# Input table of an S5 layer: its powers stored by group instead of by time step

## The chip, the cores and the metric

The kernel runs on one core of a Trainium2 chip. The metric is device time in microseconds (us), the median of the timed runs. The engines are TensorE (PE, with its weight loads PEld), VectorE (DVE), ScalarE (ACT), GpSimd (POOL) and SyncE (SP). Here POOL and SP mostly issue transfers (DMA).

## The reference, cut to what matters

A two-layer backbone on 1024 latent tokens with 256 context tokens and 1024 channels. Layer 0 has 48 groups of a bidirectional S5 recurrence (16 channels and 64 complex states per group and direction) beside an FNet part; layer 1 has pooling and a short convolution. What the change touches is the S5 recurrence of layer 0:

```
lam_bar = exp(lam * step)
b_bar   = ((lam_bar - 1) / lam)[..., None] * complex(b_re, b_im)
bu      = einsum('btgh,gph->btgp', u, b_bar)        # input to the state
s[t]    = lam_bar * s[t-1] + bu[t]                  # scan over time, both directions
y       = einsum(s.real, c_re) - einsum(s.imag, c_im)
```

All arithmetic is float32; large products are made of three products of exact high and low parts.

## The kernel before, in words

Time is cut into chunks of 8 steps. For a chunk the state's input is one matrix product: the chunk's 8 x 16 inputs times a matrix that holds, for every channel h and step s, B scaled by the power of lam_bar that belongs to s. A group's matrix has 128 columns (16 h x 8 s) and 128 rows (two directions x 64 states), for the real and the imaginary part.

`s5_prelim` (from L401) makes the powers `pw`, shaped [128, 4, 9, 48]: real part, two sums, imaginary part; powers 0 to 8; groups. Its inner function `tables(0)` copies powers 0 to 7 on ScalarE into `pwb`, six copies of 64 x 384 (three parts, two directions; one direction with the powers reversed). `tables(1)` makes `pwc` and `acf` in the same way.

`bl_task` (L493) takes four groups at a time; there are twelve such tasks. Its vector part is five VectorE operations of 128 x 512: a product into `blp`, two products into `bl`, a subtraction and an addition in `bl`. The three products read `pwb` through `W` (L502), a view [4 groups, 16 h, 8 s] in which h has step zero, and B through a view in which s has step zero. Its tensor part transposes `bl` on TensorE (L515, eight transposes into `pt`), evacuates it on ScalarE to `bltw` and stores it with a POOL transfer to `bltd`, from which `bl_load` (L964) takes it later as `blt`. `bl` has two buffers. `cl_task` (L521) does likewise for the output matrices, with `pwc`.

The order of the work is written out by hand (`manual_schedule`); each engine runs its instructions in that order. In `layer0`, from L972, a loop over six channel tiles m makes the S5 inputs: 48 products of 512 columns for the latent tokens (L360, into `acc`) and 24 of 256 columns for the context (into `uc`). Tiles 0 and 1 have their long products done before the loop; from m = 2 on the weights' high and low parts are made one tile ahead (`whi` on ScalarE, `wlo` on VectorE). `fill` (L949) is called between the products, five times per tile from m = 2 on and once at the end of m = 1: it runs the tensor part of the task started two calls before and then starts the vector part of a new one. The twelve `bl_task`s come first, then the twelve `cl_task`s. `tables(0)` stands before this loop (L923); `tables(1)` stands in it at m = 1 (L985), and the memory of the `bl` tiles is free only after it.

Behind the loop come the chunk inputs (`bl_mm`, L1018, with loads of `blt` and `ub` on the SP queue), the scan over chunks on VectorE, beside gate projections on TensorE, the S5 outputs, FNet, and then the projections of the rest of layer 0 and of layer 1.

Of the kernel before, what the change touches and what calls it, by code (L numbers as in the profile page):

```python
# [9 lines left out]
F32 = mybir.dt.float32  # L10
# [4 lines left out]
PSUM = bass.MemoryType.PSUM  # L15
DRAM = bass.MemoryType.DRAM

P = 128
# [9 lines left out]
NG = 48  # L28
EPS = 1e-6

# ------------------------------------------------------------------ constants that depend on shapes
# [17 lines left out]
def fold_index():  # L49
    """Order of the 512 time steps of the folded half: t = 8 j + s, held as s * 128 + j."""  # L50
    lin = list(range(128, 576)) + list(range(0, 64))
    return np.array([8 * (i % 128) + i // 128 for i in lin])
# [130 lines left out]
class Builder:  # L183
# [8 lines left out]
    # ---------------------------------------------------------------- small helpers  # L192
    def tick(self):
        """Between small dependent operations, the larger ones that wait for their turn (a number: that many later)."""
        self.cnt -= 1
        if self.inter and self.cnt == 0:
            self.cnt = -1000000
            while self.inter:
                x = self.inter.pop(0)
                if isinstance(x, int):  # L200
                    self.cnt = x
                    break
                x()
# [44 lines left out]
    # ---------------------------------------------------------------- streamed weights  # L248
# [51 lines left out]
    def w_issue(self, upto=-1):  # L300
        """Loads: those that the ring has room for or that have a place of their own, and all up to the given one."""
        while self.issued < len(self.jobs):
            i = self.issued
            t = self.place.get(i)
            if t is None:
                if (self.live == self.R or self.hold) and i > upto:
                    break
                t = self.wp.tile([P, 1024], F32, tag="raw", name="raw", bufs=self.R)
                self.live += 1
            self.nc.sync.dma_start(t[:, :self.jobw[i]], self.jobs[i])  # L310
            self.raw[i] = t
            self.issued += 1
# [12 lines left out]
    def w_split(self, name, eng=None, hi=None, lo=None, parts=1, c0=0, c1=None):  # L325
        """The stationary tile's exact high and low parts (columns c0 .. c1, of those that were left)."""
        if name in self.split:
            if c0 == 0:
                return self.split[name]
            hi, lo = self.split[name]  # L330
        i, raw = self.w_raw(name)
        w = self.jobw[i]
        if hi is None:
            hi = self.wp.tile([P, 1024], F32R, tag="whi", name="whi", bufs=2)
        if lo is None:
            lo = self.wp.tile([P, 1024], F32R, tag="wlo", name="wlo", bufs=2)
        for c in range(parts):
            sl = slice(max(c0, w // parts * c), min(c1 or w, w // parts * (c + 1)))
            self.act(hi[:, sl], raw[:, sl])
            self.sub(lo[:, sl], raw[:, sl], hi[:, sl].bitcast(F32), eng)  # L340
        if c1 is None:
            self.w_done(i)
        self.split[name] = (hi, lo)
        return hi, lo
# [6 lines left out]
    # ---------------------------------------------------------------- main product  # L351
    def mm3(self, outs, hi, lo, rhs, nk, hook=None):
        """outs: [(psum, first col, end col)]; rhs(k) -> (hi, lo) full-width tiles."""
        for j, k in enumerate(range(nk) if isinstance(nk, int) else nk):
            w = slice(k * P, k * P + P)
            rh, rl = rhs(k)
            last = j == (nk if isinstance(nk, int) else len(nk)) - 1
            for i, (a, b) in enumerate(((hi, rh), (hi, rl), (lo, rh))):
                for (p, c0, c1) in outs:
                    self.nc.tensor.matmul(p, a[:, w], b[:, c0:c1], start=(j == 0 and i == 0), stop=(last and i == 2))  # L360
            if hook is not None:
                hook(j)
# [8 lines left out]
    # ---------------------------------------------------------------- accurate exp on DVE  # L371
# [28 lines left out]
    # ---------------------------------------------------------------- S5 tables  # L400
    def s5_prelim(self, tp, s5s, raw):  # L401
# [41 lines left out]
        # (lam_bar - 1) / lam  # L443
# [17 lines left out]
        def inputs():  # L461
            """B times (lam_bar - 1) / lam, and the sum of its parts: the operations, one by one."""
# [12 lines left out]
        # by direction: real part, imaginary - real, real + imaginary; coefficients of the scan  # L475
        self.pwb = self.gp.tile([P, 3, 8, NG], F32, name="pwb")
# [3 lines left out]
        def tables(i):  # L480
            for ri in range(3):
                if i == 0:
                    self.act(self.pwb[0:64, ri], pw[0:64, ri, 0:8][:, ::-1])
                    self.act(self.pwb[64:128, ri], pw[64:128, ri, 0:8])
                else:
                    self.act(self.pwc[0:64, ri], pw[0:64, ri])
                    self.act(self.pwc[64:128, ri], pw[64:128, ri][:, ::-1])
# [5 lines left out]
    def bl_task(self, b, hf):  # L493
        """Chunk input matrices of 4 groups, transposed, to DRAM: (vector part, tensor part)."""
# [4 lines left out]
        def dve():  # L499
            p = self.gt.tile([P, 4, 16, 8], F32, tag="blp", name="blp", bufs=1)  # L500
            B = [x[:, g4].unsqueeze(3).to_broadcast([P, 4, 16, 8]) for x in (self.bbs, self.bb[:, 0], self.bb[:, 1])]
            W = [self.pwb[:, i, :, g4].rearrange("p s g -> p g s").unsqueeze(2).to_broadcast([P, 4, 16, 8])  # L502
                 for i in range(3)]
# [17 lines left out]
    def cl_task(self, b, hf):  # L521
        """Chunk output matrices and kernel strips by lag of 4 groups, to DRAM."""
# [45 lines left out]
    # ---------------------------------------------------------------- modulation  # L568
    def ada_mm(self, l, ch, ps=None, p=0, last=True):
        """Columns 256 ch .. + 256 of silu(cond) @ w, in four parts by rows of w, as rows 2 p, 2 p + 1 of 32."""  # L570
# [16 lines left out]
    def ada_fin(self, parts, row):  # L587
        """The parts' sums, by channel on partitions; shift and gate: + b, scale: (1 + . + b) * g."""
# [15 lines left out]
    def ada_part(self, l, ch):  # L604
        """One part's products; eight parts share a bank, whose end is ada_end."""
# [23 lines left out]
    # ---------------------------------------------------------------- 1 / rms, broadcast to all partitions  # L629
    def ss_mm(self, ps, sq, first=True, last=True):  # L630
        """ps[i]: [2, w] += the sums over the partitions of sq's columns w i .. w i + w."""
# [12 lines left out]
    def rstd_r(self, row, n, pool):  # L644
        """A row of sums of squares -> 1 / rms, tokens on partitions."""
# [5 lines left out]
    def rstd_a(self, ss, n, pool):  # L651
        """ss: tiles [128, 128 n] that add up to the sums over channel tiles of squares -> 1 / rms, tokens on partitions."""
# [19 lines left out]
    def rstd_d(self, sd, h, w, dg):  # L672
        """Diagonals of 1 / rms of w 128-token tiles."""
# [4 lines left out]
    def rstd_p(self, dg, w):  # L678
        """1 / rms on all partitions, in PSUM."""
# [13 lines left out]
    # ================================================================ the program  # L693
# [34 lines left out]
    def hl_tile(self, name, dt=F32R):  # L728
        """One of the places hh0 .. hh7, hl0 .. hl7: of high and low parts, or of float32 data before or after."""
        return self.hlp.tile([P, T], dt, tag=name, name=name)  # L730

    def layer0(self, es):
# [71 lines left out]
        def mod_0():  # L804
            """The first channel tile from 1 / rms in PSUM, by halves."""
# [24 lines left out]
        def warm(n):  # L830
            """Keeps the tensor engine's clock up while the inputs come."""
# [96 lines left out]
        # ---- S5 inputs, with the S5 matrices made behind them  # L928
# [83 lines left out]
        # ---- chunk inputs, and the rest of the S5 matrices  # L1012
# [45 lines left out]
        # ---- the scan over chunks: the context's in pairs, the rest's behind the FNet inputs and the gate projection  # L1058
# [14 lines left out]
        def tree(c, l):  # L1073
            """Pairs of the context's chunks -> one."""
# [10 lines left out]
        def step(*ci):  # L1085
            """Chunk states i of groups half c, for all (c, i); the products and sums of a half held in v[0]'s first rows
            once the context's states are done with."""
# [52 lines left out]
        # ---- S5 outputs, by token; transposed back, split for the GLU product, and times the gate  # L1140
# [4 lines left out]
        # the FNet's constants, inputs and first products take the place of the chunk states that are done with  # L1145
# [113 lines left out]
        # ---- FNet  # L1259
# [60 lines left out]
        # ---- GLU  # L1320
# [28 lines left out]
    # ---------------------------------------------------------------- residual, sums of squares  # L1349
    def out_proj(self, wname, l, rhs, passes, prep, finish, wbuf, scr, korder, nxt=()):  # L1350
        """xl += gate * (y @ w), pass by pass over the tokens; finish(p, first, end, sums of squares), in parts,
        runs behind the next pass. wbuf(m): where to hold the parts of w; scr(name, i): [128, 512] of scratch."""
# [43 lines left out]
    def norm_part(self, c0, c1, ss, scr, emit, kn=KD):  # L1396
        """Parts of a normalisation of columns c0 .. c1; emit(k, 1 / rms), k < kn."""
# [15 lines left out]
    def layer1(self, es):  # L1413
# [105 lines left out]
        def y_split(k):  # L1519
            """The high part to yh; the low part to the place of the tile before it."""  # L1520
# [102 lines left out]
```

## Time and profile before

| | us |
|---|---|
| median of 3 timed runs | 947.31 |
| the three runs | 943.85, 947.31, 948.86 |
| span of the profiled execution | 943.4 |
| own time of the profiled execution | not shown; the nearest timed run is 943.85 |
| TensorE, VectorE, ScalarE, POOL busy | 888.9, 589.4, 315.9, 93.8 |

The span runs from the first to the last instruction of one execution. A busy time is the sum of an engine's instructions in it; it does not say which of them the end waited for. The chain that ended last does: it is followed back from the last instruction, at each step to what released it. Start times are counted from the start of the span.

### The profile page before, as it was taken

What the parts mean: (1) busy time and instruction counts of PE and PEld (TensorE: products, weight loads), DVE (VectorE), ACT (ScalarE), POOL (GpSimd) and SP (SyncE); (2) the same over time, 40 slices, a digit from 0 to 9 for tenths busy, and PEclk for the clock granted to TensorE, in tenths of its full rate; (3) what the DMA queues carried; (4) which work ended last, traced back from release to release, by engine and by line L of the source; (5) the groups of instructions that cost most, each with busy time, mean ns of one, the idle gap of its engine ahead of it and who ended that gap; (6) DMA issues with size and microseconds to landing.
All of it is one profiled execution on the core that took longest, in us unless ns stands there. A gap on an engine that the chain in (4) does not pass through costs nothing.

```text
span 943.4 us, 13977 instructions
## 1 busy us (share of the span) xinstructions
PE 888.9 (94%) x5432; PEld 725.6 (77%) x5432; DVE 589.4 (62%) x1563; ACT 315.9 (33%) x535; POOL 93.8 (10%) x91
## 2 busy tenths in 40 slices
PE   8998788898999958899999999999999999999996
PEld 3666566677777748887888999877888888888995
DVE  7788998767999996656367476254321343335355
ACT  5546331346212109744342244212111222233110
POOL 0002221131221303200043000100000000000000
PEclk9999999999999988999999999999999999999998
DMA  9734557994455466931162010201111111111022
GB/s 348 283 134 144 186 171 206 261 358 157 157 201 187 185 210 192 312 138 40 67 263 94 1 42 4 79 23 57 56 38 52 45 45 45 50 64 44 1 90 89
DMA packets 57601, 120.75 MB, mean 128 GB/s; under 512 B 5248, under 2 KB 30000, under 8 KB 57408
## 3 DMA queue, kind: packets, MB, share of 16 engines
q1 hardware_dynamic: 50672, 96.06, 30.2%
q0 software_dynamic: 6864, 23.81, 8.0%
q8 instruction: 42, 0.69, 0.3%
q14 instruction: 23, 0.19, 0.1%
HBM read 95.83 MB, written 24.02 MB: 127 GB/s over the span
## 4 chain that ended last, share of the span: by engine, by line
PE 62%; DVE 24%; DMA 6%; ACT 5%; issue 1%; SPq 1%; DVEq 0%; POOL 0%; ACTq 0%; POOLq 0%
PE acc L360 53%; DVE va L206 11%; DVE bl L206 4%; DVE vb L206 2%; DMA mt<-zd 2%; PE acc L867 2%; ACT vb L231 1%; DMA zd<-z 1%; DVE blp L206 1%; PE yps L1189 1%; ACT sy L231 1%; DVE xt L206 1%; PE pps L1509 1%; DMA ub<-ud 1%; PE rsb L682 1%
## 5 line engine op out<-in xcount | busy, mean ns | idle before, releaser
L360 PE MATMUL acc<-hh,whi 128*128 128x512 f32 (+1 forms) x672 | 211.8, 388 | 1.4 <-ACT whi L231 1.4
L360 PE MATMUL acc<-hl,whi 128*128 128x512 f32 (+1 forms) x672 | 207.1, 382 | 0.0
L360 PE MATMUL acc<-hh,wlo 128*128 128x512 f32 (+1 forms) x672 | 206.7, 381 | 0.1
L360 PEld LDWEIGHTS acc<-hh,whi 128*128 128x128 f32 x672 | 122.7, 188 | 30.4 <-issue 5.8
L360 PEld LDWEIGHTS acc<-hh,wlo 128*128 128x128 f32 x672 | 125.1, 188 | 25.9 <-DVE wlo L206 0.5
L360 PEld LDWEIGHTS acc<-hl,whi 128*128 128x128 f32 x672 | 125.2, 188 | 25.5
L206 DVE TENSOR_TENSOR wlo<-raw,whi 128x1024 fp32r<-128x1024 f32 (+2 forms) x47 | 52.3, 1118 | 50.9 <-ACT whi L231 50.9
L231 ACT ACTIVATE whi<-raw 128x1024 fp32r<-128x1024 f32 (+2 forms) x55 | 53.9, 986 | 50.2 <-issue 29.0
L206 DVE TENSOR_TENSOR va<-va 128x48 f32<-128x48 f32 (+1 forms) x258 | 55.9, 218 | 0.4
L227 DVE SCALAR_TENSOR_TENSOR xl<-acc,adac,xl 128x256 f32<-128x256 f32 (+1 forms) x48 | 27.3, 570 | 41.6 <-PE acc L360 41.3
L360 PE MATMUL acc<-yh,hh 128*128 128x256 f32 (+1 forms) x144 | 46.3, 321 | 0.0
L360 PE MATMUL acc<-hh,wl 128*128 128x256 f32 (+1 forms) x144 | 46.1, 320 | 0.0
L360 PE MATMUL acc<-hh,wh 128*128 128x256 f32 (+1 forms) x144 | 46.0, 320 | 0.0
L360 PE MATMUL acc<-yl,hh 128*128 128x256 f32 (+1 forms) x144 | 45.8, 318 | 0.0
L360 PE MATMUL acc<-yh,hl 128*128 128x256 f32 (+1 forms) x144 | 45.7, 317 | 0.0
L360 PE MATMUL acc<-hl,wh 128*128 128x256 f32 (+1 forms) x144 | 45.6, 317 | 0.0
L1189 PE MATMUL yps<-cl,sy 128*128 128x128 f32 x192 | 32.3, 295 | 12.7 <-ACT sy L231 12.7
L206 DVE TENSOR_TENSOR va<-va,acf 128x96 f32<-128x96 f32 x127 | 38.7, 305 | 0.2
L1189 PEld LDWEIGHTS yps<-cl,sy 128*128 128x128 f32 x192 | 28.0, 210 | 13.2 <-ACT sy L231 13.0
L231 ACT ACTIVATE hh<-xl 128x256 f32<-128x256 f32 (+1 forms) x24 | 11.7, 489 | 70.2 <-DVE xl L227 70.2
L206 DVE TENSOR_TENSOR va<-vb,acf 128x96 f32<-128x96 f32 x127 | 34.2, 269 | 0.2
L1026 PE MATMUL vps<-ub,blt 128*64 128x160 f32 x192 | 28.3, 301 | 3.9 <-DMA ub<-ud 2.5
(264 smaller groups left out, 1630.7 us busy)
## 6 DMA issues: line engine op xcount, KB each, us to landing
raw<-in_ada SPq DMA_DIRECT2D x44, 512.0 KB, 6.2
raw<-in_win SPq DMA_DIRECT2D x38, 512.0 KB, 3.6
raw<-in_wout SPq DMA_DIRECT2D x16, 512.0 KB, 3.5
bltd<-bltw POOLq DMA_DIRECT2D x12, 512.0 KB, 3.2
blt<-bltd SPq DMA_DIRECT2D x12, 512.0 KB, 8.6
cl<-cld POOLq DMA_DIRECT2D x12, 512.0 KB, 6.4
cld<-cl SPq DMA_DIRECT2D x18, 256.0 KB, 4.3
ub<-ud SPq DMA_DIRECT2D x12, 384.0 KB, 7.4
```

The lines of the kernel that those rows point to most:

```text
L206: (eng or self.nc.vector).tensor_tensor(out, a, b, op=op)
L227: self.nc.vector.scalar_tensor_tensor(out, a, s, b, op0=op0, op1=op1)
L231: self.nc.scalar.activation(out, a, func, **kw)
L360: self.nc.tensor.matmul(p, a[:, w], b[:, c0:c1], start=(j == 0 and i == 0), stop=(last and i == 2))
L682: self.nc.tensor.matmul(p2[:, P * i:P * i + P], self.ones, dg[:, i], start=True, stop=True)
L867: nc.tensor.matmul(acc[m][h], a[:, w], b[:, 512 * h:512 * h + 512], start=(k == 0 and i == 0), stop=(k == 7 and i == 2))
L1026: nc.tensor.matmul(ps[0:64, o], blt[:, ri, g, 0:64], ub[:, g, 0:160], start=True, stop=True)
L1189: nc.tensor.matmul(ps[:, o], sy[:, ri, g], cl[:, ri, g], start=False, stop=(ri == 1))
L1509: nc.tensor.matmul(ps, pwt[:, i], pd[:, 4 * h:4 * h + 4].rearrange("p s j -> p (s j)"), start=True, stop=True)
```

## The change

The table `pwb` is laid out [part, group, step] instead of [part, step, group]. The six copies that fill it write through a rearranged view, so that their output has a step of eight elements from one group to the next; the vector part of `bl_task` reads it without a rearrangement. The numbers computed are the same. Comments were dropped as well, which is left out here.

```diff
-        self.pwb = self.gp.tile([P, 3, 8, NG], F32, name="pwb")
+        self.pwb = self.gp.tile([P, 3, NG, 8], F32, name="pwb")
...
         def tables(i):
             for ri in range(3):
                 if i == 0:
-                    self.act(self.pwb[0:64, ri], pw[0:64, ri, 0:8][:, ::-1])
-                    self.act(self.pwb[64:128, ri], pw[64:128, ri, 0:8])
+                    self.act(self.pwb[0:64, ri].rearrange("p g s -> p s g"), pw[0:64, ri, 0:8][:, ::-1])
+                    self.act(self.pwb[64:128, ri].rearrange("p g s -> p s g"), pw[64:128, ri, 0:8])
...
             B = [x[:, g4].unsqueeze(3).to_broadcast([P, 4, 16, 8]) for x in (self.bbs, self.bb[:, 0], self.bb[:, 1])]
-            W = [self.pwb[:, i, :, g4].rearrange("p s g -> p g s").unsqueeze(2).to_broadcast([P, 4, 16, 8])
-                 for i in range(3)]
+            W = [self.pwb[:, i, g4].unsqueeze(2).to_broadcast([P, 4, 16, 8]) for i in range(3)]
             self.mul(p, B[0], W[0])
             self.mul(bl[:, 0], B[2], W[2])
             self.mul(bl[:, 1], B[1], W[1])
             self.sub(bl[:, 0], p, bl[:, 0])
             self.add(bl[:, 1], p, bl[:, 1])
```

## Rows read from the trace of the kernel before

**Rows 1.** The page's busy times: engine, us, share of the span, instructions.

```profile
PE   888.9 (94%) x5432; PEld 725.6 (77%) x5432; DVE 589.4 (62%) x1563; ACT 315.9 (33%) x535; POOL 93.8 (10%) x91
```

**Rows 2.** The page's chain that ended last, by line.

```profile
PE acc L360 53%; DVE va L206 11%; DVE bl L206 4%; DVE vb L206 2%; DMA mt<-zd 2%; PE acc L867 2%; ACT vb L231 1%; DMA zd<-z 1%; DVE blp L206 1%; PE yps L1189 1%; ACT sy L231 1%; DVE xt L206 1%; PE pps L1509 1%; DMA ub<-ud 1%; PE rsb L682 1%
```

**Rows 3.** Stretch: us, busy PE, PEld, DVE, ACT, POOL; TensorE clock, DMA share, GB/s.

```profile
80.00:150.00 70.00, 58.08 (x344) 45.18 (x344) 67.14 (x81) 26.83 (x52) 19.46 (x25) 1.00 0.61 185
150.00:220.00 70.00, 59.92 (x788) 46.59 (x788) 52.35 (x125) 29.66 (x67) 11.55 (x16) 1.00 0.99 302
238.00:353.00 115.00, 105.87 (x643) 78.77 (x641) 115.00 (x726) 20.51 (x43) 21.86 (x14) 0.97 0.55 193
```

**Rows 4.** Waits, 78 to 240 us: us in total, times, longest.

```profile
DVE cl L206 <- DMA cld<-cl: 10.1, 5, 3.8
...
PE pt L515 <- DVE bl L206: 9.2, 10, 1.7
```

**Rows 5.** Timeline of VectorE: start, us, operation, count, idle time before it.

```profile
85.93 1.12 DVE L206 TENSOR_TENSOR blp<-bbs,pwb 128x512 f32<-128x512 f32 x1 [1.26 <-ACT acf L231]
...
135.31 1.21 DVE L206 TENSOR_TENSOR wlo<-raw,whi 128x1024 fp32r<-128x1024 f32 x1
136.45 1.09 DVE L206 TENSOR_TENSOR blp<-bbs,pwb 128x512 f32<-128x512 f32 x1
...
140.64 0.94 DVE L206 TENSOR_TENSOR cbs<-cb 128x768 f32<-128x768 f32 x1
```

**Rows 6.** Groups of VectorE, 0 to 240 us: count, busy us, mean ns, idle before.

```profile
L206 DVE TENSOR_TENSOR bl<-bb,pwb 128x512 f32<-128x512 f32 x24 | 24.9, 1083 | 0.0
L206 DVE TENSOR_TENSOR cl<-cb,pwc 128x576 f32<-128x576 f32 x24 | 17.1, 753 | 10.5 <-DMA cld<-cl 10.1 <-issue 0.4
L206 DVE TENSOR_TENSOR bl<-blp,bl 128x512 f32<-128x512 f32 x24 | 15.5, 689 | 0.0
L206 DVE TENSOR_TENSOR blp<-bbs,pwb 128x512 f32<-128x512 f32 x12 | 13.1, 1089 | 1.5 <-ACT acf L231 1.3
...
L206 DVE TENSOR_TENSOR rsd<-cst,rs 128x512 f32<-128x512 f32 x2 | 1.4, 692 | 0.1
```

**Rows 7.** Groups of ScalarE, 0 to 420 us, in the same columns.

```profile
L231 ACT ACTIVATE bltw<-pt 128x512 f32<-128x512 f32 x24 | 13.8, 600 | 36.1 <-PE pt L515 21.0 <-issue 7.7 <-DMA bltd<-bltw 4.2
...
L231 ACT ACTIVATE vb<-vps 128x480 f32<-128x480 f32 x12 | 12.4, 1037 | 3.1 <-PE vps L1027 3.1
...
L231 ACT ACTIVATE vb<-vps 128x160 f32<-128x160 f32 x12 | 5.9, 492 | 0.0
...
L231 ACT ACTIVATE pwb<-pw 64x384 f32<-64x384 f32 x6 | 3.1, 520 | 0.1
...
L231 ACT ACTIVATE utc<-uc 128x256 f32<-128x256 f32 x6 | 2.3, 381 | 0.0
```

**Rows 8.** Timeline of ScalarE between `pwb` and `acf`.

```profile
75.31 3.18 ACT L231 ACTIVATE pwb<-pw 64x384 f32<-64x384 f32 x6
...
85.26 0.64 ACT L231 ACTIVATE acf<-pw 128x48 f32<-128x48 f32 x4
```

**Rows 9.** Timeline of TensorE: the first products of m = 2, the last transposes of `bl`.

```profile
80.73 0.73 PE L360 MATMUL acc<-hh,whi 128*128 128x512 f32 x2 [1.37 <-ACT whi L231]
...
91.22 0.62 PE L360 MATMUL acc<-hl,whi 128*128 128x512 f32 x2
91.69 0.63 PE L360 MATMUL acc<-hh,wlo 128*128 128x512 f32 x2
...
140.25 1.23 PE L515 MATMUL pt<-cst,bl 128*128 128x128 f32 x8 [1.29 <-DVE bl L206]
141.24 0.72 PE L360 MATMUL acc<-hh,whi 128*128 128x512 f32 x2
```

**Rows 10.** Transfers, 75 to 240 us: queue, count, KB each, median us to landing.

```profile
bltd<-bltw POOLq DMA_DIRECT2D x12, 512.0 KB, 3.2
blt<-bltd SPq DMA_DIRECT2D x12, 512.0 KB, 8.6
```

## The prediction

> **What bounds the kernel now.** I read the page's busy times first. TensorE (PE) is busy 94% of the span [rows 1]. From that alone work on VectorE (DVE) would be free. The chain that ended last says otherwise: among its lines are "bl L206" with 4% and "blp L206" with 1% [rows 2]. These are the five VectorE operations of a `bl_task`, so about 47 us of the chain are the very operations that the diff touches. Next I asked for busy times by stage [rows 3]. In 80 to 150 us VectorE is busy 67.1 of 70 us and TensorE 58.1. From 150 to 220 the DMA share is 0.99. From 238 to 353 (the scan) VectorE is busy all the time. So the change sits in a stage that VectorE bounds, with TensorE close behind and transfers next.
>
> The waits agree: transposes `pt` wait 9.2 us for `bl`, in ten places [rows 4]. In VectorE's timeline the first task starts at 85.93, after a wait for ScalarE (ACT) and its `acf`; the last one starts at 136.45, and `cbs`, the first operation of the `cl` tasks, at 140.64 [rows 5]. Between lie 12 tasks and three `wlo` (136.45 - 135.31 = 1.14 us from start to start): 54.71 - 3.42 = 51.29, or 4.27 us per task.
>
> **Part 1: the reads of pwb.** Three of a task's five operations read `pwb`; over 12 tasks that is 36, each on 512 elements. They take 1083 ns (24 into `bl`) and 1089 ns (12 into `blp`); the two subtractions and additions, also on 512 elements, take 689 ns [rows 6]. Before, W's innermost step is a whole row of 48 groups (192 bytes); after, eight neighbouring elements are read, then read again for the next h. B's innermost step is zero in both kernels. Could that zero step be the slow part? Two rows say no: `rsd` reads one operand with a zero step innermost and takes 692 ns for 512; `cl<-cb,pwc` does so too and takes 753 ns for 576 [rows 6]. So each operation should fall to about 689 ns: 24 x 394 + 12 x 400 ns = 14.3 us less VectorE work. A task falls from 4.27 to 3.08 us; I use 3.1. The other end of this term is no gain at all (a rival below).
>
> [...]
>
> **Part 2: the writes of pwb.** The six ScalarE copies now write with a step of eight elements (32 bytes). Now they write contiguously and take 520 ns for 64 x 384 [rows 7]. The trace has no write with this step, but it has writes with a step of 192 bytes: `vb<-vps` 128 x 480 takes 1037 ns, while contiguous copies from PSUM take 600 (`bltw<-pt`, 512) and 381 (`utc<-uc`, 256), 0.855 ns per element, so some 573 for 480: 0.97 ns more per element. On 160 elements it is 492 ns, against 299: 1.2 ns per element [rows 7]. I take 0.97, of the row nearest in size: 384 x 0.97 = 0.37 us, times six 2.2 us. The ends are 0 and 2.8 us (1.2 ns). Below nothing is excluded: the number of elements is the same and the write is contiguous now.
>
> This is not hidden. ScalarE's queue holds, from 75.31 on: six `pwb`, `ut`, `whi`, `utc`, `ut`, six `pwc`, four `acf` that end at 85.9 [rows 8]. TensorE waits 1.37 us for that `whi` before the next channel tile's product at 80.73 [rows 9], and VectorE waits for `acf` before the first task. So both start 2.2 us later, TensorE at 82.9 and VectorE at 88.1.
>
> [...]
>
> **Part 3: what is late next.** With VectorE at 3.1 us per task, five tasks and one `wlo` (1.14 us from start to start) make 16.6 us per channel tile; now they make 22.5. TensorE's own work per channel tile, from starts in its timeline [rows 9]: 48 products of 512 columns, two per 0.465 us, 11.2 us; 24 of 256 columns at half of that, 0.12 each, 2.9; five sets of eight transposes, 4.5, at 0.9 each (140.25 to 141.24 is 0.99, and it begins from a standstill). That is 18.6 us. So the bound passes from VectorE to TensorE, and TensorE sets the gain.
>
> The last set of transposes starts at 140.25 now. From 80.73 until then TensorE has 126 long products (29.3 us), 48 short (5.8) and 11 sets of transposes (9.9), 45.0 us; the other 14.5 of 59.5 us are stalls. After the change I replay it. VectorE starts a task, TensorE can take it 2.6 us later (3.8 now, from 136.45 to 140.25, less 1.2). Tasks start at 88.1, 92.3 (after a `wlo`), 95.4, 98.5, 101.6; they are ready at 90.7, 94.9, 98.0, 101.1, 104.2. TensorE arrives at 89.9, 94.4, 97.2, 101.8, 104.1. It stalls 0.8 + 0.5 + 0.8 + 0 + 0.1 = 2.2 us, then VectorE is ahead. So the last set starts at 82.9 + 45.0 + 2.2 = 130.1: 10.1 us earlier.
>
> VectorE itself reaches `cbs` about 12 us earlier (14.3 less 2.2), so the `cl` tasks wait for nothing there. Everything after hangs on TensorE and on the `cl` tasks: products, `ud` stores, `ub` and `blt` loads, the saturated stretch, the scan, then TensorE alone. Nothing in it starts at a fixed time; the weight loads are issued when buffers come free. I carry the whole 10.1 us to the end. Can the DMA engines take it? They are busy 0.61 x 70 = 42.7 us of the 70 before 150 [rows 3]; in 60 us that is 0.71.
>
> **The sum.** The profiled execution has a span of 943.4 us; no time of its own is shown, and the nearest timed run, 943.85, leaves 0.4 around it. By its own time I expect 943.85 - 10.1 = 933.8. The median of the three runs is 947.31, 3.5 above that run; the gain is in device work and should not depend on it, so I forecast 947.31 - 10.1 = 937.2. With writes between 0 and 2.8 us the gain is 12.3 to 9.5; with transposes at 1.1 us a set another 1.3 is lost. With the runs' own spread its range is 934 to 941.
>
> **Rivals.** (a) *The transfers give part of it back.* From 150 to 220 they are saturated, VectorE waits 10.1 us for `cld<-cl` [rows 4], and `cld`, `zd`, `blt` and `ub` share the SP queue. If the denser stage before makes the first `blt` and `ub` loads meet stores still under way, one loaded landing more is paid: `blt` takes 8.6 us where `bltd`, in the emptier stage, takes 3.2 [rows 10]; 5.4 us lost, gain 4.7, time 942.6. For: that stretch has no slack. Against: its producers all move by the same 10 us.
>
> (b) *The write is much dearer than its neighbours* (slower than before). Its place is the six ScalarE copies ahead of `whi` and `acf`; each us more there delays TensorE and VectorE alike. It eats the gain of 12.3 from 2.05 us more per copy, 5.3 ns per element; at 3 us per copy the time is 947.31 + 18 - 12.3 = 953. Against: the dearest strided copy here pays 1.2 ns per element.
>
> (c) *The reads don't get faster*, the change not doing what its layout suggests: then only 2.2 us are added, 949.5. Against: the two rows with zero steps.
>
> (d) *The write costs nothing*: 935.0, on the forecast's side.
>
> **Chances.** Forecast with (d) 0.74; (a) 0.17, of which about a third keeps more than 0.5%; (b) 0.04; (c) 0.05. About 0.5%, 4.7 us, can be told from no change. So faster 0.79 (0.74 and a third of (a)), same 0.16 ((a)'s rest and (c)), slower 0.05 (most of (b) and the worst of (c)). The range, 934 to 943.5, takes in the ends of the write's cost and (a).
>
> **What would show it.** `bl<-bb,pwb` and `blp<-bbs,pwb` at 0.67 to 0.72 us. `pwb<-pw` at 0.85 to 1.0 us. `acf` ending at about 88. `pt` waiting for `bl` at most 3 us in total, and TensorE busy over 95% from 90 to 130. The last transposes of `bl` at about 130, `cbs` at about 129. The scan's start some 10 us earlier, and equal stage lengths after it. Wrong would be: reads still above 0.9 us, writes above 1.5, or a stretch of saturated transfers that ends less than 6 us earlier although the transposes ended 10 earlier.

## The result: 935.21 us, 1.2% below

The changed kernel takes 935.21 us (median, 934.26 to 937.35) against 946.47 for the kernel before in the same set of runs (four of each, the three runs above among them): a ratio of 0.9882 (95% interval 0.9855 to 0.991), 11.3 us less. A second set gave 937.43 against 946.78, 0.9894 (0.9872 to 0.9915). Executions in a slow state, such as two of the eleven of the kernel before in that set, which took 1002 us, are left out of all comparisons. The profiled executions have spans of 943.4 and 932.7 us, 10.7 apart; the one after took 934.52 us in all. The forecast was 937.2, 10.1 us less, with a range of 934 to 943.5.

The groups that the diff touches, after: VectorE's three kinds of operation in a `bl` task, then ScalarE's copies into the table (columns as in [rows 6]).

```profile
L206 DVE TENSOR_TENSOR bl<-bb,pwb 128x512 f32<-128x512 f32 x24 | 15.4, 683 | 0.0
L206 DVE TENSOR_TENSOR bl<-blp,bl 128x512 f32<-128x512 f32 x24 | 15.4, 683 | 0.0
L206 DVE TENSOR_TENSOR blp<-bbs,pwb 128x512 f32<-128x512 f32 x12 | 8.3, 689 | 1.5 <-ACT acf L231 1.3
```

```profile
L231 ACT ACTIVATE pwb<-pw 64x384 f32<-64x384 f32 x6 | 5.6, 928 | 0.1
```

The reads of `pwb` fell from 1083 and 1089 ns to 683 and 689: all five operations of a task now take the same time. That is 24 x 0.400 + 12 x 0.400 = 14.4 us of VectorE work. The copies rose from 520 to 928 ns [rows 7], 2.45 us in all.

VectorE's timeline after: the first task, the last one, and the end of the tasks.

```profile
88.32 0.69 DVE L206 TENSOR_TENSOR blp<-bbs,pwb 128x512 f32<-128x512 f32 x1 [1.25 <-ACT acf L231]
...
125.83 0.68 DVE L206 TENSOR_TENSOR blp<-bbs,pwb 128x512 f32<-128x512 f32 x1
...
128.84 0.95 DVE L206 TENSOR_TENSOR cbs<-cb 128x768 f32<-128x768 f32 x1
```

It starts 2.39 us later than before (85.93) and reaches `cbs` 11.8 us earlier (140.64) [rows 5]. TensorE in the same stretch, with the first products of tile m = 2, three sets of transposes, and the last one:

```profile
83.13 0.75 PE L360 MATMUL acc<-hh,whi 128*128 128x512 f32 x2 [3.83 <-ACT whi L231]
83.72 0.85 PE L360 MATMUL acc<-hl,whi 128*128 128x512 f32 x2
84.39 1.22 PE L360 MATMUL acc<-hh,wlo 128*128 128x512 f32 x2
85.41 1.05 PE L360 MATMUL acc<-hh,whi 128*128 128x512 f32 x2
...
91.43 0.62 PE L360 MATMUL acc<-hh,wlo 128*128 128x512 f32 x2
91.89 1.03 PE L514 MATMUL pt<-cst,bl 128*128 128x128 f32 x8
...
95.58 1.04 PE L514 MATMUL pt<-cst,bl 128*128 128x128 f32 x8
...
98.24 1.23 PE L514 MATMUL pt<-cst,bl 128*128 128x128 f32 x8 [0.22 <-DVE bl L206]
...
130.52 1.03 PE L514 MATMUL pt<-cst,bl 128*128 128x128 f32 x8
```

There is one wait for `bl` left, 0.22 us; there were ten with 9.2 us [rows 4]. The last set starts at 130.52, 9.73 us earlier than 140.25 [rows 9]. In 90 to 130 us TensorE is busy 39.78 of 40, where it was 32.94 before (columns: stretch, its length, TensorE busy and count, granted clock, DMA share, GB/s):

```profile
83.00:85.00 2.00, 1.87 (x6) 0.73 0.57 166
85.00:87.00 2.00, 2.00 (x6) 0.50 0.93 188
87.00:90.00 3.00, 3.00 (x13) 0.94 0.99 324
90.00:130.00 40.00, 39.78 (x239) 1.00 0.71 219
```

The first two rows show something that the forecast did not have: after the wait of 3.83 us the granted clock is 0.73 on the mean of 83 to 85 us and 0.50 in 85 to 87; in 87 to 90 its mean is 0.94.

What follows moves as a block. The stretch of saturated transfers, ten us earlier than in [rows 3], has nearly the same row (columns as there):

```profile
140.00:210.00 70.00, 62.01 (x768) 48.64 (x760) 51.59 (x125) 30.62 (x68) 11.51 (x15) 0.95 0.97 296
```

And the scan's second half begins 10.45 us earlier, first in the kernel before, then after:

```profile
226.86 1.83 DVE L206 TENSOR_TENSOR tr<-vb,acf 128x768 f32<-128x768 f32 x2 [4.13 <-ACT vb L231]
```

```profile
216.41 1.83 DVE L206 TENSOR_TENSOR tr<-vb,acf 128x768 f32<-128x768 f32 x2 [3.83 <-ACT vb L231]
```

From there to the end the spans need 716.5 and 716.3 us. So of the 10.7 us, 9.73 are won before the last transposes of `bl`, 0.72 between them and the scan, and 0.2 after it.

### The profile page after: what moved, and what is told of

The parts are those of the page before. It is cut to its first block, busy times and chain, and to the rows that moved or that the text cites. A ratio compares the mean times of both kernels' runs of the same rounds, so it can differ in the third digit from the quotient of the medians.

```text
span 932.7 us, 13977 instructions
## 1 busy us (share of the span) xinstructions
PE 886.7 (95%) x5432; PEld 728.5 (78%) x5432; DVE 574.6 (62%) x1563; ACT 318.2 (34%) x535; POOL 94.1 (10%) x91
## 4 chain that ended last, share of the span: by engine, by line
PE 62%; DVE 23%; ACT 6%; DMA 6%; issue 1%; SPq 1%; DVEq 0%; ACTq 0%
PE acc L360 53%; DVE va L206 11%; DVE bl L206 3%; DVE vb L206 2%; DMA cld<-cl 2%; ACT sy L231 2%; DMA ub<-ud 2%; PE acc L866 2%; DMA mt<-zd 1%; ACT vb L231 1%; DVE xt L206 1%; DVE blp L206 1%; DVE cl L206 1%; PE pps L1508 1%; PE rsb L681 1%
## 5 line engine op out<-in xcount | busy, mean ns | idle before, releaser
L206 DVE TENSOR_TENSOR va<-va 128x48 f32<-128x48 f32 (+1 forms) x258 | 58.0, 226 | 0.4
L1188 PE MATMUL yps<-cl,sy 128*128 128x128 f32 x192 | 32.6, 296 | 12.7 <-ACT sy L231 11.3
L206 DVE TENSOR_TENSOR va<-va,acf 128x96 f32<-128x96 f32 x127 | 34.2, 269 | 0.2
```

The costliest lines, as they stand in the source:

```text
L206: (eng or self.nc.vector).tensor_tensor(out, a, b, op=op)
L1188: nc.tensor.matmul(ps[:, o], sy[:, ri, g], cl[:, ri, g], start=False, stop=(ri == 1))
```

## The experiments

Profiles differ by some 3 us before any edited instruction has run. For comparisons across kernels I count from the first `chh` of the context (68.9 us in the kernels before and after), which stands ahead of all edits' effects but those of the last run, to the start of the last set of `bl` transposes; call it the distance. It is 71.3 us before and 61.6 after.

**Reads alone.** The copies write the same memory contiguously; only the reading is new.

```diff
-  self.act(self.pwb[0:64, ri].rearrange("p g s -> p s g"), ...)
+  self.act(self.pwb[0:64, ri].rearrange("p g s -> p (g s)").rearrange("p (s g) -> p s g", s=8), ...)
```

> The copies write the same memory contiguously, as before, and the tasks read eight neighbours, as after (the powers then stand in the wrong order, so the numbers computed differ from the reference). Theory (the reads give 14.3 us of VectorE's time, the strided writes take back what they delay): pwb<-pw at 0.52 us, reads at 0.69, TensorE starts tile m = 2 at 80.7 instead of 83.1, its last transposes of bl come at about 128 instead of 130.5, time 2 to 3 us below the changed kernel: 932 to 933.5, ratio to before 0.985 to 0.987. Rival (the writes' delay is hidden, since TensorE would wait for VectorE anyway): the time of the changed kernel, 935.

933.07 us, ratio 0.986 (0.9839 to 0.9882). In its groups the copies are back at 522 ns and the reads stay fast; in its timelines TensorE starts m = 2 after a short wait and the last transposes come early.

```profile
L206 DVE TENSOR_TENSOR bl<-bb,pwb 128x512 f32<-128x512 f32 x24 | 15.4, 684 | 0.0
```

```profile
L231 ACT ACTIVATE pwb<-pw 64x384 f32<-64x384 f32 x6 | 3.1, 522 | 0.1
```

```profile
80.33 0.73 PE L360 MATMUL acc<-hh,whi 128*128 128x512 f32 x2 [1.39 <-ACT whi L231]
...
127.72 1.03 PE L514 MATMUL pt<-cst,bl 128*128 128x128 f32 x8
```

Distance 59.2, 2.4 less than with the strided writes: the copies' 2.45 us, not hidden. By the medians it is 2.1 us below the first set of the changed kernel; the two intervals (0.9839 to 0.9882 and 0.9855 to 0.991) overlap, so the size rests on the trace.

**Writes alone.** Strided copies as after; the tasks read the same memory with a step of 48 elements.

```diff
-  W = [self.pwb[:, i, g4].unsqueeze(2)...]
+  W = [self.pwb[:, i].rearrange("p g s -> p (g s)").rearrange("p (s g) -> p s g", s=8)[:, :, g4]
+       .rearrange("p s g -> p g s").unsqueeze(2)... for i in range(3)]
```

> The copies write with a step of eight elements, as after, and the tasks read the same memory with a step of 48, as before (values in the wrong order). Theory: pwb<-pw at 0.93, reads still at 1.08, VectorE bounds the stage as before and starts 2.4 us later: last transposes at 142.7, time 2.5 us above the kernel before, 949, ratio 1.002 to 1.004. Rival (the faster reads come from the table's tile and not from the step between elements): reads at 0.69 and a time of 935.

949.2 us, ratio 1.0029 (1.0011 to 1.0046): slower than before by 0.3%, which is 2.7 us (1 to 4.4 by the interval). Its groups and its last transposes:

```profile
L206 DVE TENSOR_TENSOR bl<-bb,pwb 128x512 f32<-128x512 f32 x24 | 25.0, 1089 | 0.0
```

```profile
141.90 1.23 PE L515 MATMUL pt<-cst,bl 128*128 128x128 f32 x8 [1.28 <-DVE bl L206]
```

Distance 73.9, 2.6 more than before. The tile and its place are the same as after, and the reads take 1089 ns where they took 683: it is the step of 48 elements that makes them slow here. The two halves add up: -12.1 (reads) + 2.6 (writes) = -9.5, and both together gave -9.7.

**One operation less on VectorE.** The changed kernel without `self.add(bl[:, 1], p, bl[:, 1])`.

```diff
             self.sub(bl[:, 0], p, bl[:, 0])
-            self.add(bl[:, 1], p, bl[:, 1])
```

> The changed kernel without the last addition of each bl task (its imaginary part is then only one of two terms): 0.6 us less VectorE work per task, 7.2 us in all. Theory (after the change TensorE bounds this stage): cbs starts some 7 us earlier, at about 121.7, but the last transposes stay within 0.7 us of 130.5 and the time within 1 us of 935. Rival (VectorE still bounds it): the transposes come 7 us earlier and the time is 928.

934.88 us, ratio 0.9877 (0.9856 to 0.9898): no change from 0.9882 and 0.9894. Distance 60.9, 0.7 less. The rival, VectorE still being the bound, would have it 7 us less and falls. One part of the expectation missed: `cbs` comes 2.0 us earlier on this scale, not 7. Its waits say why:

```profile
DVE bl L206 <- PE pt L513: 4.4, 3, 2.5
```

`bl` has two buffers, and VectorE now waits for TensorE to have transposed the one before last. The order of waiting has turned round.

**Copies ahead of whi, or behind it.** `tables(0)` is moved behind the `whi` of tile 2; TensorE no longer waits for the copies, VectorE's first task still does.

```diff
-        tables(0)
         inputs = inputs()
...
                 self.w_split(names[2])
+                tables(0)
```

> The changed kernel with tables(0) issued behind the whi of tile 2 and not ahead of it: TensorE no longer waits for the copies, VectorE's first bl task still does (acf comes last on ScalarE). Theory (TensorE's delay and its slow clock after the wait are hidden behind VectorE's late start): TensorE starts m = 2 at about 79.4, at the full clock, waits some 4 us for the first transposes instead, the third set of transposes comes at 98.2 as now, the last at 130.5, time within 1 us of the changed kernel. Rival (the price of the writes is paid through TensorE's late start, 3.8 us, and the slow clock, 1.7 us): 930 to 932.

937.17 us, ratio 0.9911 (0.9886 to 0.9937): as the changed kernel beside it, 937.43. TensorE's wait only moved, from `whi` to the first transposes, and its granted clock fell to 0.50 there (columns as above). The profile names no releaser for that wait (`issue`); VectorE's last two operations on this set of `bl` start at 92.59, and the transposes of the set's first half begin as the first of the two, of some 0.7 us, ends:

```profile
92.59 1.28 DVE L206 TENSOR_TENSOR bl<-blp,bl 128x512 f32<-128x512 f32 x2
```

```profile
93.48 1.94 PE L514 MATMUL pt<-cst,bl 128*128 128x128 f32 x8 [4.54 <-issue]
95.07 1.20 PE L360 MATMUL acc<-hh,whi 128*128 128x512 f32 x2
```

```profile
90.00:92.00 2.00, 0.00 (x0) 1.00 0.85 231
92.00:94.00 2.00, 0.52 (x3) 0.55 0.94 319
94.00:96.00 2.00, 2.00 (x9) 0.50 0.60 180
96.00:98.00 2.00, 2.00 (x6) 0.50 0.80 268
```

Distance 62.9, 1.1 more than the 61.8 of the changed kernel beside it. Of this, 0.4 is VectorE's own: its first task starts 19.8 us after the first `chh`, against 19.4. The rest was not separated; the slow clock lies there, and behind it no transposes wait for `bl` any more. So freeing TensorE alone buys nothing: VectorE's late start is enough to hold the stage. The reverse, VectorE freed alone, was not run. In the changed kernel TensorE, once started, waits only 0.22 us for `bl`, so with its own start as late as it is, little could have come of that.

**Keeping TensorE busy during the wait.** Twelve unused products in the changed kernel.

```diff
+            if m == 1:
+                warm1 = self.ps("m", "warm1")
+                for _ in range(12):
+                    nc.tensor.matmul(warm1[:, 0:P], self.ones, self.ones, start=True, stop=True)
```

> The changed kernel with 12 products of ones by ones (their result is not used) between the context's products of tiles 0 and 1, so that TensorE does not stand still for 3.8 us before m = 2. Theory: the granted clock stays at 1.00 from 83 to 88, the 30 products ahead of the first transposes take 7.0 us instead of 8.8, and TensorE waits for VectorE there instead: last transposes within 0.5 us of 130.5, time within 1 us of the changed kernel. Rival (the slow clock's 1.7 us reach the end): 933 to 934 and last transposes at 128.8.

935.25 us, ratio 0.9867 (0.9844 to 0.9891), against 0.9894 (0.9872 to 0.9915) for the changed kernel beside it; the intervals overlap, and the two profiles differ by 1.8 us already at the first `chh`. Its granted clock stays at 1.00, and the 30 products ahead of the first transposes take 82.08 to 89.99, with a wait of 0.32 us, instead of 83.13 to 91.89. Like for like, from the first product to the start of the last pair, it is 6.97 us (82.08 to 89.05) instead of 8.30 (83.13 to 91.43); before, it was 6.98 (80.73 to 87.71). So the slow clock cost 1.3 us. Then TensorE waits for `bl` again:

```profile
83.00:85.00 2.00, 1.95 (x9) 1.00 0.91 242
85.00:87.00 2.00, 2.00 (x11) 1.00 0.96 227
```

```profile
82.08 0.75 PE L360 MATMUL acc<-hh,whi 128*128 128x512 f32 x2 [1.12 <-ACT whi L231]
...
89.05 0.63 PE L360 MATMUL acc<-hh,wlo 128*128 128x512 f32 x2
89.99 1.16 PE L514 MATMUL pt<-cst,bl 128*128 128x128 f32 x8 [0.32 <-issue]
...
97.20 1.23 PE L514 MATMUL pt<-cst,bl 128*128 128x128 f32 x8 [0.51 <-DVE bl L206]
...
129.50 1.03 PE L514 MATMUL pt<-cst,bl 128*128 128x128 f32 x8
```

By the third set of transposes the two are level: it starts 29.34 us after the first `chh` here and 29.35 after it in the changed kernel. Distance 61.6, as without the unused products (61.6 and 61.8). The slow clock cost TensorE time that it would have spent waiting for VectorE.

**The other loop order.** The copies write contiguously and read `pw` with a step of 48 elements.

```diff
-  self.act(self.pwb[0:64, ri].rearrange("p g s -> p s g"), pw[0:64, ri, 0:8][:, ::-1])
+  self.act(self.pwb[0:64, ri], pw[0:64, ri, 0:8][:, ::-1].rearrange("p s g -> p g s"))
```

> The changed kernel with the loops of the six copies in the other order: they write pwb contiguously and read pw with a step of 48 elements. If the price is one per element that has no neighbour next to it, on whichever side: pwb<-pw at 0.85 to 0.95 us and the time of the changed kernel. If it is the writes' alone: 0.52 us and 2 us less.

936.22 us, ratio 0.9885 (0.9861 to 0.991), as the changed kernel. The copies take 882 ns:

```profile
L231 ACT ACTIVATE pwb<-pw 64x384 f32<-64x384 f32 x6 | 5.3, 882 | 0.1
```

So these copies pay on whichever side the step is. Against the 522 ns of the contiguous ones (reads alone), over 384 elements, it is 1.06 ns per element for the write with 32 bytes (928 ns) and 0.94 for the read with 192 bytes (882 ns).

**Copies in ScalarE's idle time.** The changed kernel with the six copies issued from 63.7 us on, where ScalarE waits for VectorE. `pwb(ri, h)` issues one of them; the tiles of the tables are made earlier for it, which is left out here.

```diff
-  ... mod_l(7), ctx_r, first(5), first(6), 4, ctx_b,
-      1, ctx_mod(0, 1), 1, ctx_mod(2, 3), first(7), 1, ctx_mod(4, 5), 1, ctx_mod(6, 7)]
+  ... mod_l(7), ctx_r, pwb(0, 0), pwb(0, 1), pwb(1, 0), first(5), first(6), 4, ctx_b,
+      1, ctx_mod(0, 1), pwb(1, 1), 1, ctx_mod(2, 3), pwb(2, 0), first(7), 1, ctx_mod(4, 5), pwb(2, 1), 1, ctx_mod(6, 7)]
...
-        tables(0)
```

> The changed kernel with the six copies into pwb issued earlier on ScalarE, three after the context's row of 1 / rms and one after each of three context modulations, where ScalarE waits for VectorE. Theory (what is left of the writes' price is the delay of whi and acf): whi of tile 2 at about 76.5, TensorE starts m = 2 at 79.3 without a wait and at the full clock, VectorE's first task at about 83.5, last transposes at about 125, time 5 to 6 us below the changed kernel: 929 to 930.5, ratio 0.982 to 0.984. Rival 1 (the transfers of 140 to 210 set the scan's start): the transposes come 5 us earlier but the scan less than 2, time above 933. Rival 2 (the copies in the gaps delay the context's chain by as much): TensorE's start at 83 as now, 935.

930.58 us, ratio 0.9831 (0.9814 to 0.9849): faster than both kernels; the interval does not touch the changed kernel's first one, 0.9855 to 0.991. Its ScalarE, VectorE and TensorE:

```profile
63.69 2.92 ACT L231 ACTIVATE pwb<-pw 64x384 f32<-64x384 f32 x3
...
73.15 0.96 ACT L231 ACTIVATE pwb<-pw 64x384 f32<-64x384 f32 x1
...
76.04 1.06 ACT L231 ACTIVATE whi<-raw 128x1024 fp32r<-128x1024 f32 x1
```

```profile
83.02 0.69 DVE L206 TENSOR_TENSOR blp<-bbs,pwb 128x512 f32<-128x512 f32 x1
```

```profile
78.83 0.62 PE L360 MATMUL acc<-hh,whi 128*128 128x512 f32 x2
...
125.19 1.03 PE L516 MATMUL pt<-cst,bl 128*128 128x128 f32 x8
```

TensorE starts m = 2 and VectorE its first task without a wait, 10.4 and 14.6 us after the first `chh`, against 14.2 and 19.4 after the change. Three copies now run before that `chh`, in time in which ScalarE would have waited: it still waits 1.83 us there. The copies are as dear as ever (961 ns on the mean), but the end no longer waits for them. Distance 56.8, 4.9 less than after; the median is 4.6 less. Both rivals fall: the transfers passed the 5 us on (the scan's second half starts 142.1 us after the first `chh`, against 147.5), and the context's chain was hardly held up (its last `chh` starts 6.2 us after its first, against 6.0).

In all ten profiles the time from the last `bl` transposes to the end lies between 800.6 and 804.4 us, while their start ranges from 125.2 to 141.9. That spread is smaller than the 10 us of the gain: nothing behind them took it back.

## Why the prediction was right

**Reads** (forecast 14.3 us): 14.4. The writes-alone run shows that the step does it. B is read with its zero step in the changed kernel too, at 683 ns, so that step is innocent (rival c).

**Writes** (forecast 2.2, ends 0 to 2.8): 2.45, 1.06 ns per element. The neighbour that was chosen, with a step of 192 bytes and 0.97 ns per element, stood for one of 32 bytes; rivals (b) and (d) were both wrong by the same row.

**Not hidden**: both engines started 2.4 us later, and reads-alone gave 2.4 us back. The reason is more exact now. The two delays lie side by side. With TensorE's taken away VectorE's holds the stage, as the whi-first run shows; that TensorE's would hold it with VectorE's taken away is only argued, from the 0.22 us that TensorE still waits for `bl`. Reads-alone and the early copies take both away, and there the gain arrives.

**The bound passes to TensorE**: so it did; taking 7 us more from VectorE moved the last transposes by 0.7 us and left the time as it was. The replay had 2.2 us of stalls and none of the slow clock. Measured were 0.22 us of stalls and, from 83.13 to 91.89, 8.76 us for 30 products that the replay put at 7.0. Of the difference 1.3 us is the slow clock's; the other 0.4 stands in the run with unused products as well, at full clock. The two errors are one thing: TensorE, slowed, came later and found `bl` ready. The last transposes came at 130.5 for 130.1.

**The rest is carried through** (rival a, 5.4 us lost in the transfers): nothing was lost. The share of the DMA engines in the stretch of 70 us is 0.97 after, 0.99 before, and it began 10 us earlier. VectorE's waits in the `cl` tasks did not vanish, though: for `cld<-cl` they are 12.0 us (78 to 230 us) where they were 10.1.

The gain by the medians, 11.3, is 1.2 us above the forecast. Part of that is won between 131 and 216 us (0.72), where the `cl` tasks had a VectorE 11.8 us ahead instead of 9.7; which of their waits gave it was not separated. The rest is within the runs' spread of 3 to 5 us. The time, 935.21 for 937.2, is 2.0 below the forecast; the other 0.8 is that the kernel before has its median at 946.47 with a fourth run, and not at 947.31.

One reading in the sum was wrong, without harm to the forecast. The prediction took 943.85 for the own time of the profiled execution, whose span is 943.4. Every other execution on record lasts at least 1.7 us longer than its span (934.52 against 932.7 for the one after), so by an estimate from these the profiled one took 945.1 or more. Less 10.1 that is 935.0, where the prediction had 933.8; the profiled execution after took 934.52.

## What to carry to other kernels

A table that is filled once and read many times belongs in the order of its readers (here each of 36 reads became 0.40 us shorter and each of six copies 0.41 us longer); price both sides by strided rows of the same trace, since the copy that turns it round was not free. Then place that copy where its engine waits for another: here this was worth another 4.6 us on top of the 11.3 of the new layout. (Of the copies' 5.6 us, 3.1 stood in the path of the kernel before as well; what the move alone would have given there was not run.) And when an engine stops being the bound, ask which one is next: it sets how much of the saved work reaches the end, here 9.7 of 14.4 us; 2.4 went to the writes, the other 2.3 were more than TensorE could follow.

## What the runs showed of the hardware

TensorE's granted clock fell from 1.00 to 0.50 after it had stood still for 3.83 us (after; 0.50 in 85 to 87 us) and 4.54 us (whi first; 0.50 in 94 to 98); before, with 1.37 us in the same place, it stayed at 1.00 (80 to 90), and so it did in the run with unused products in between (1.12 us; 83 to 90). From what length of wait on it falls was not shown. The slow clock cost 1.3 us between the first and the last pair of the 30 products after the first of these (8.30 us against 6.97). In the second execution of the same kernel that was profiled, after a wait of 3.78 us, the clock was 0.50 in 83 to 88 us and cost 2.3 (83.91 to 93.19, 9.28 us). In neither did it reach the last transposes, which came 61.6 and 61.8 us after the first `chh`, and 61.6 where the clock had not fallen.
